# Scaling whole tiles with one VectorE instruction, empty instructions at ScalarE's head, and the first two loads on SyncE, in a row softmax on one core

## The chip, the cores and the metric

The kernel runs on one core of a Trainium2 chip. VectorE, ScalarE and SyncE are engines of the core, each with its own program; ScalarE and SyncE here also issue the transfers, each to a queue of its own. The metric is the device time of one execution in microseconds. The trace also gives a span, from the first to the last instruction of the program; the time is 1.7 to 1.8 us above it in every run here.

## The reference

The input is 16 x 1024 x 512 fp32, seen as 16,384 rows of 512. Each row gets a softmax of x / 2:

```python
x_scaled = x / 2.0
x_max = np.max(x_scaled, axis=-1, keepdims=True)
exp_x = np.exp(x_scaled - x_max)
return (exp_x / np.sum(exp_x, axis=-1, keepdims=True)).astype(np.float32)
```

That is 33.55 MB in and 33.55 MB out, and little arithmetic for each byte.

## The kernel before

Each of the 128 partitions holds 128 rows, in ten tiles: one of 3 rows, one of 7, seven of 15 and a last one of 13. In SBUF they lie in one arena of 100 rows, so tiles 8 and 9 reuse the places of earlier tiles and wait for their stores. Below, "row" is a row of 512 within a partition.

```python
PLAN = [
    ([3], 0), ([4, 3], 3), ([5] * 3, 10), ([5] * 3, 25), ([5] * 3, 40), ([5] * 3, 55),
    ([5] * 3, 70), ([5] * 3, 85), ([5] * 3, 0), ([5, 4, 4], 15),
]                       # chunks of each tile, and its place in the arena
LAG = 2                 # a chunk is scaled two chunks after its maximum
FUSED = {1, 2, 3}       # tiles that one tensor_mul scales per chunk
```

SyncE loads tile 0; ScalarE loads the rest. Tile 1's load is in three pieces: all but its last row, then the last row of 126 partitions, then that of two.

```python
if t == 0:
    nc.sync.dma_start(out=sb(t), in_=dram(xf, t)).then_inc(ld[t], 16)
elif t == SPREAD:                       # SPREAD = 1
    r = tiles[t][1] - 1
    for p, q, lo, hi in ((0, P, 0, r), (0, 126, r, r + 1), (126, P, r, r + 1)):
        nc.scalar.dma_start(...).then_inc(ld[t], 16)
else:
    nc.scalar.dma_start(out=sb(t), in_=dram(xf, t)).then_inc(ld[t], 16)
```

VectorE takes the negated maximum of a chunk. ScalarE takes the exponential of each row in place and adds up its sum. VectorE then takes the reciprocals and scales, and SyncE stores a tile once all of it is scaled.

```python
def do_mul(k):
    ...  # reciprocal of the chunk's sums, waits for its exponentials
    if t in FUSED:
        nc.vector.tensor_mul(chunk, chunk, recip broadcast along the row)
        return
    for r in range(c):
        nc.vector.tensor_scalar_mul(out=arena[:, a + r], in0=arena[:, a + r],
                                    scalar1=recip[:, b + r : b + r + 1])
```

The loads of tiles 0 and 1 stand ahead of the barrier with which the program begins, all other work behind it.

## Time and profile before

| | before |
|---|---|
| time | 161.64 us (161.61 to 161.68, 3 runs) |
| span of the profiled run | 159.9 us |
| VectorE (DVE) busy | 131.6 us, last instruction over at 144.7 us |
| ScalarE (ACT) busy | 94.4 us |
| transfers | 67.1 MB, first packet at 1.0 us, last at 158.6 us |
| tiles 0, 1, 2 reach VectorE | 6.71, 9.39, 18.26 us |

In the profile's row of slices, a digit is a fortieth of the span and gives the busy share in tenths. A transfer counts from its issue on a sequencer (SPq or ACTq) to its landing, when all its engines have reported to its semaphore. Within the chain that ended last (start in us, length, what), the piece that stands out is a load:

```profile
94.63 32.69 DMA arena<-in_x_dram
127.32 0.02 issue
127.34 2.82 DVE negmax L105
```

The last tile's load was issued at 94.63 and landed 32.7 us later; behind it come 17 us of VectorE and the last store. So loads, VectorE's tail and stores are linked here, with the transfers full throughout.

### The profile page before, as it was taken

To read this page: it belongs to the slowest core of one execution; us is meant where nothing else is said; L and a number is where in the kernel's file an instruction comes from. 1 tells how busy PE (TensorE), PEld (TensorE's weight loads), DVE (VectorE), ACT (ScalarE), POOL (GpSimd) and SP (SyncE) were. 2 spreads that over 40 slices of the span, in tenths; PEclk is the share of its full clock that TensorE was granted. 3 is DMA by queue.
4 is the path that set the end of the run, shared out by engine and by line. 5 is a ranking of instruction groups with operands and counts; after the bars stand their busy time and mean duration, and the time that the engine had idled before them with its cause. 6 is when DMAs were issued, how large, how long until landed. Compare 5 with 4: busy or idle time off the path is not lost.

```text
span 159.9 us, 476 instructions
## 1 busy us (share of the span) xinstructions
DVE 131.6 (82%) x153; ACT 94.4 (59%) x257; POOL 0.2 (0%) x4
## 2 busy tenths in 40 slices
DVE  0376499999999999999999999999999799992000
ACT  0369176768448547766688666786667948650000
POOL 0000000000000000000000000000000000000000
DMA  7998999999998989899999999998999998989993
GB/s 278 466 396 377 447 424 407 446 475 376 418 484 377 484 377 484 377 484 407 448 423 446 423 438 453 402 461 387 452 448 438 396 484 377 484 384 476 431 426 133
DMA packets 3028, 67.13 MB, mean 420 GB/s; under 512 B 337, under 2 KB 337, under 8 KB 721
## 3 DMA queue, kind: packets, MB, share of 16 engines
q1 hardware_dynamic: 1584, 34.34, 50.1%
q10 hardware_dynamic: 1440, 32.77, 48.1%
q14 instruction: 4, 0.02, 0.0%
HBM read 33.55 MB, written 33.55 MB: 420 GB/s over the span
## 4 chain that ended last, share of the span: by engine, by line
DVE 58%; DMA 31%; issue 0%; DVEq 0%; ACT 0%
DMA arena<-in_x_dram 31%; DVE negmax L105 30%; DVE arena L125 13%; DVE arena L118 13%; DVE recip L114 1%; DVEq L218 0%; ACT arena L144 0%
## 5 line engine op out<-in xcount | busy, mean ns | idle before, releaser
L144 ACT ACTIVATE arena<-arena,negmax 128x512 f32<-128x512 f32 x128 | 90.7, 710 | 42.5 <-DVE negmax L105 42.5
L105 DVE TENSOR_REDUCE negmax<-arena 128x5 f32<-128x2560 f32 (+2 forms) x27 | 72.1, 2675 | 12.2 <-DMA arena<-in_x_dram 12.2
L125 DVE TENSOR_SCALAR arena<-arena,recip 128x512 f32<-128x512 f32 x91 | 37.8, 482 | 0.7
L144 ACT ACTIVATION_READ_ACCUMULATOR arena<-arena,negmax 128x1 f32 x128 | 23.9, 187 | 0.0
L118 DVE TENSOR_TENSOR arena<-arena,recip 128x2560 f32<-128x2560 f32 (+2 forms) x8 | 21.0, 2625 | 0.3
L114 DVE RECIPROCAL recip<-sums 128x5 f32<-128x5 f32 (+2 forms) x27 | 4.8, 176 | 0.0
L144 ACT ACT_TABLE_LOAD x1 | 1.3, 1283 | 5.0 <-issue 5.0
L207 POOL MEMSET const-bfloat16-1.0<- 128x1 bf16 x1 | 0.1, 103 | 0.0
L207 POOL MEMSET const-uint8-127<- 128x1 uint8 x1 | 0.1, 103 | 0.0
L207 POOL MEMSET const-float32-1.0<- 128x1 f32 x1 | 0.1, 100 | 0.0
L207 POOL MEMSET const-float32-0.0<- 128x1 f32 x1 | 0.1, 99 | 0.2 <-issue 0.2
## 6 DMA issues: line engine op xcount, KB each, us to landing
arena<-in_x_dram ACTq DMA_DIRECT2D x7, 3840.0 KB, 42.9
out_dram<-arena SPq DMA_DIRECT2D x7, 3840.0 KB, 24.0
arena<-in_x_dram ACTq DMA_DIRECT2D x1, 3328.0 KB, 32.7
out_dram<-arena SPq DMA_DIRECT2D x1, 3328.0 KB, 14.2
out_dram<-arena SPq DMA_DIRECT2D x1, 1792.0 KB, 17.0
arena<-in_x_dram ACTq DMA_DIRECT2D x1, 1536.0 KB
arena<-in_x_dram SPq DMA_DIRECT2D x1, 768.0 KB, 6.7
out_dram<-arena SPq DMA_DIRECT2D x1, 768.0 KB, 15.5
```

The lines of the kernel that those rows point to most:

```text
L105: nc.vector.reduce_max(out=negmax[:, b : b + c], in_=arena[:, a : a + c], axis=mybir.AxisListType.X, negate=True,)._wait_ge(ld[t], 48 if t ...
L114: nc.vector.reciprocal(out=recip[:, b : b + c], in_=sums[:, b : b + c])._wait_ge(s_exp, k + 1).then_inc(s_rec, 1)
L118: nc.vector.tensor_mul(out=arena[:, a : a + c], in0=arena[:, a : a + c], in1=recip[:, b : b + c].unsqueeze(2).to_broadcast([P, c, D]),)._w ...
L125: ins = nc.vector.tensor_scalar_mul(out=arena[:, a + r], in0=arena[:, a + r], scalar1=recip[:, b + r : b + r + 1],)
L144: ins = nc.scalar.activation(out=arena[:, a + r], in_=arena[:, a + r], func=mybir.ActivationFunctionType.Exp, bias=negmax[:, b + r : b + r ...
L207: nc = _bacc.Bacc("TRN2", target_bir_lowering=False, num_devices=1)
```

## The change

The intent, as the code shows it: fewer and larger instructions on VectorE (a maximum for 8 or 7 rows instead of 5, one scaling instruction for a tile, two for the last), both first tiles loaded from one queue, ahead of the others, and ScalarE held back a little by 48 empty instructions, so that the first tiles have the transfer engines to themselves. A tile in PLAN now has the chunks for its maxima, the groups that one instruction scales, and its place. The diff, cut to its core (constants that stand twice in it are shown once):

```diff
 PLAN = [
-    ([3], 0), ([4, 3], 3), ([5] * 3, 10), ([5] * 3, 25), ...
+    ([3], [3], 0), ([4, 3], [7], 3), ([8, 7], [15], 10), ([8, 7], [15], 25),
+    ([8, 7], [15], 40), ([8, 7], [15], 55), ([8, 7], [15], 70), ([8, 7], [15], 85),
+    ([8, 7], [15], 0), ([5, 4, 4], [9, 4], 15),
 ]
+AHEAD = 48
+FIRST = 2
...
-            if t == 0:
-                nc.sync.dma_start(out=sb(t), in_=dram(xf, t)).then_inc(ld[t], 16)
-            elif t == SPREAD:
+            queue = nc.sync if t < FIRST else nc.scalar
+            if t == SPREAD:
...
+            for p, q, lo, hi in parts:
+                queue.dma_start(...).then_inc(ld[t], 16)
...
-    def do_mul(k):
-        t, b, c, a = chunks[k]
+    def do_mul(j):
+        t, b, c, a, k = groups[j]
...
-        for r in range(c):
-            ins = nc.vector.tensor_scalar_mul(...)
+        nc.vector.tensor_mul(
+            out=arena[:, a : a + c],
+            in0=arena[:, a : a + c],
+            in1=recip[:, b : b + c].unsqueeze(2).to_broadcast([P, c, D]),
+        )._wait_ge(s_rec, j + 1).then_inc(s_mul, 1)
...
-    issue_loads(0, 2)
+    issue_loads(0, FIRST)
+    for _ in range(AHEAD):
+        nc.scalar.nop()
```

## The prediction

> **What bounds the kernel now.** I read the page first: busy shares, the 40 slices, HBM bytes.
>
> ```profile
> span 159.9 us, 476 instructions
> DVE 131.6 (82%) x153; ACT 94.4 (59%) x257; POOL 0.2 (0%) x4
> DMA  7998999999998989899999999998999998989993
> HBM read 33.55 MB, written 33.55 MB: 420 GB/s over the span
> ```
>
> The row of DMA tenths is full from the second slice to the last but one, while VectorE has 28 us to spare: the transfers are the bound. Next the stages, cut by time (columns: window, length, busy us of DVE, ACT, POOL, clock, DMA share, GB/s).
>
> ```profile
> 2.00:6.00 4.00, 0.00 (x0) 1.00 (x1) 0.00 (x0) 1.00 1.05 427
> 42.00:127.00 85.00, 83.67 (x103) 61.09 (x169) 0.00 (x0) 1.00 1.00 432
> 127.00:154.00 27.00, 17.23 (x31) 10.25 (x29) 0.00 (x0) 1.00 1.01 436
> ```
>
> In the middle DVE is busy 98% too, so it is a close second; but DVE ends at 144.7 and stores alone fill the last 14 us. That backlog is DVE's slack. The 67.1 MB at 432 GB/s take 155.3 us, so a perfect start could win only about 2 us of 161.6. Third, the DVE rows by shape, and its first waits.
>
> ```profile
> L105 DVE TENSOR_REDUCE negmax<-arena 128x5 f32<-128x2560 f32 x22 | 61.9, 2813 | 4.6 <-DMA arena<-in_x_dram 4.6
> L125 DVE TENSOR_SCALAR arena<-arena,recip 128x512 f32<-128x512 f32 x91 | 37.8, 482 | 0.7
> L118 DVE TENSOR_TENSOR arena<-arena,recip 128x2560 f32<-128x2560 f32 x6 | 16.9, 2825 | 0.2
> ...
> 6.71 1.75 DVE L105 TENSOR_REDUCE negmax<-arena 128x3 f32<-128x1536 f32 x1 [6.71 <-DMA arena<-in_x_dram]
> 9.39 3.94 DVE L105 TENSOR_REDUCE negmax<-arena 128x4 f32<-128x2048 f32 x2 [0.93 <-DMA arena<-in_x_dram]
> 18.26 2.82 DVE L105 TENSOR_REDUCE negmax<-arena 128x5 f32<-128x2560 f32 x1 [3.53 <-DMA arena<-in_x_dram]
> ```
>
> Tiles 0, 1 and 2 reach DVE at 6.7, 9.4 and 18.3 us. Last, the DMA queues while both have work. q1 is SyncE's, q10 ScalarE's. At 2.5 to 5.5 us it is load against load, at 18 to 29 us the store of tile 0 (rows of 6,144 bytes) against loads (rows of 30,720).
>
> ```profile
> q10 hardware_dynamic: 68, 0.84, 68.3%
> q1 hardware_dynamic: 65, 0.40, 32.8%
> ...
> q10 hardware_dynamic: 144, 3.93, 82.8%
> q1 hardware_dynamic: 137, 0.79, 17.1%
> out_dram<-arena SPq DMA_DIRECT2D x1, 768.0 KB, 15.5
> ```
>
> The columns are packets, MB, share. The **packet counts** of the two queues are equal, 68 to 65 and 144 to 137, while the bytes follow the row size. So a queue with small rows gets few bytes: tile 0's store needed 15.5 us for 0.79 MB.
>
> **What the Trainium skill says.** "DMA: Bandwidth & Descriptors", section "Queues, rings and completion order": an engine round-robins between queue rows at packet granularity. The counts above agree; where the page expects some 9 to 17 descriptors in a packet, this trace has one row per packet. The same page, "Why a DMA increments its semaphore by 16 and not by 1", says a copy is split over the largest number of engines up to 16 that divides its row counts: 126 rows on 14 engines, 2 rows on 2. The program's split of tile 1's last row matches; no view names the engines. "VectorE: DVE Perf Modes", section "The perf-mode tier table (the rule you actually need)": fp32 tensor_scalar in SBUF runs at 2x, tensor_tensor at 1x. The trace agrees: five L125 take 2.07 us, one L118 of the same data 2.82 us.
>
> **The change part by part.**
>
> *1. The 48 empty instructions.* The build drops them: the built program of the changed kernel has no such instruction and the same order as one built with none. Effect 0. They would have held ScalarE's loads back behind SyncE's; that is lost.
>
> *2. Scaling and chunks.* The reduces of 5, 4 and 3 rows last 2813, 2281 and 1747 ns in the table by shape, so a row of 512 costs 0.533 us; from start to start one of 5 takes 2.73 (18.26 to 20.99), so 0.07 comes on top. The tensor_tensor has the same slope (2825, 2292, 1757) and 0.08 on top; a reciprocal takes 0.20. After tile 0's reduce the new DVE program holds:
> - reduces: 125 rows x 0.533 + 19 instructions x 0.07 = 68.0 us
> - scaling: 128 rows x 0.533 + 11 x 0.08 = 69.1 us
> - 11 reciprocals x 0.20 = 2.2 us
>
> That is **139.3 us**. The 91 rows that were scaled one by one cost 0.40 each (five from 65.06 to 67.04) and now 0.533, so +12 us; 16 fewer reciprocals and 7 fewer reduces give back 3.7. A full tile costs 4.34 + 3.80 + 0.20 + 8.08 = 16.4 us of DVE against 18.2 us of DMA (7.86 MB at 432 GB/s), so DVE still keeps up in the middle, but the slack at the end is nearly used.
>
> *3. Both first tiles on SyncE.* This is the part I expect to decide. SyncE's program now runs four issues before the barrier. From the durations seen (0.38, 0.38, 0.66, 0.25 with gaps of 0.04) it is through at 1.8 instead of ScalarE's 1.48, so tile 2's load is issued at about 2.28 (1.97 before). ScalarE's first load had its first packet 2.2 us after its issue (packet records: issued 0.12, data 2.30), so tile 2's packets begin near 4.5 us. By then tile 0 is done: 0.29 MB by 2.2 us in the queue view, the other 0.50 MB at 0.41 MB per us, so 3.4 us. Of tile 1's eight 12,288-byte packets per engine (0.46 us each) two to three are through. From there on every tile-1 packet takes turns with one 30,720-byte packet of tile 2 and then of tile 3, which needs 1.14 us (128 of them in the 9.1 us of 3.93 MB at 432 GB/s, eight per engine):
> - 5 packets left of the main part: 5 x (1.14 + 0.46) = 8.0, to 12.5 us
> - then its completion packet, 9 packets of 2,048 bytes, a completion packet and, on two engines, the two-row piece with its completion: 13 turns x 1.14 + 10 x 0.08 = 15.6, to **28 us**
>
> The check on this: tile 0's store has 8 data packets of 0.23 and one completion per engine, so 8 x 1.37 + 1.14 = 12.1 us from its first packet at 18.0; its last engine reported at 30.3. In the kernel before, tile 1 was ahead of tile 2 in one queue and was there at 9.4.
>
> *The sum.* DVE runs in program order; everything after tile 0's reduce, even tile 0's scaling, stands behind tile 1. So DVE idles from about 6 to 28 us and then works without a gap: 28 + 139.3 = 167.3. I checked tiles 8 and 9: their loads are issued near 76 and 109 us, after stores that have landed by then, and are needed at 128 and 145 us. The last store (3.41 MB, nothing left to share with) takes 1.0 to its first byte, 7.9 at 432 GB/s and 0.4 to report: 9.3, so 176.6. The end took 1.0 (158.93 to 159.9), which gives a span of 177.6. The time is 1.7 above the span (161.64 against 159.9): **179 us**.
>
> **Rivals.**
> - *Tile 1 is early after all.* If the empty instructions do reach the chip and last about 0.1 us each, or if a small row is not made to wait a turn, tile 1 lands near 8. Then DVE starts freely only with tile 2 at 17 to 18 us and has 133.5 us from there (139.3 less 5.8 of tile 1's reduces, tile 0's scaling and reciprocal): 18 + 133.5 + 9.3 + 1.0 + 1.7 = 163.5, or 162.5 with tile 2 at 17. Within 2%. For it speaks that somebody put the empty instructions there; against it the built program and the equal packet counts.
> - *Small rows share a turn.* If two 2,048-byte rows go in one turn, the tail has some five turns fewer, tile 1 lands near 22.5 and the time is 173.5. No view shows 2,048-byte rows competing, so I keep this in the range.
> - *DMA stays the bound and hides the rest* (161 to 162): this needs a DVE chain that ends by about 149, so tile 1 by 10. It is the old bound, and part 3 takes it away.
> - *Faster.* Tile 0 comes earlier (about 4 us, was 6.7), but tile 2 cannot come more than some 1.5 us earlier, and DVE has more work. I see no way to 2%.
>
> **Range and chances.** The end moves one to one with tile 1's arrival. With 22 to 31 us for it, and 1 us for the rest, the time is 172 to 183; I stretch the low side to 169 for a shorter tail or a later tile 2. The first rival has about 9%, faster 1%, slower the rest.
>
> **What would show it.** Right: tile 1's first reduce starts near 28 us with a DVE wait of about 20 us on a load; queue q1 moves little over 100 GB/s after 5 us and less later; after that DVE has no wait over 1 us to its end near 167; the scaling rows of 7680 elements take about 8.1 us; the DMA row has gaps late in the run; loads of ScalarE start at 2.3 us. Wrong: many empty instructions on ScalarE or loads issued after 5 us; tile 1's reduce before 12 us; a DVE wait on tiles 8 or 9; DVE ending much before the last store is issued.

## The result, and the profile after

The changed kernel takes **176.88 us** (median of 4 runs, 176.11 to 178.01); the kernel before takes 161.66 beside it. The ratio is 1.0947, with a 95% interval of 1.0888 to 1.1007. Ratios here are the mean time of one kernel's fast runs over that of the other's from the same rounds, so not quite the ratio of the medians. The output is correct.

The page of the changed kernel, the lines that answer to those of before:

```profile
span 175.1 us, 365 instructions
DVE 141.2 (81%) x42; ACT 92.8 (53%) x257; POOL 0.2 (0%) x4
DMA  7999999999999999999989999999397059559795
HBM read 33.55 MB, written 33.55 MB: 383 GB/s over the span
```

The transfers now have holes in the last third, and VectorE was busy for only 10 us more while the span grew by 15. No empty instructions ran: the trace has 365 instructions, 111 fewer than before, and VectorE alone has 111 fewer (42 for 153). ScalarE's 257 would not show it, since they leave out what only a sequencer runs. The timeline of VectorE (start, length, instruction, idle time ahead of it and what ended it) shows where it stood idle:

```profile
4.47 1.75 DVE L129 TENSOR_REDUCE negmax<-arena 128x3 f32<-128x1536 f32 x1 [4.47 <-DMA arena<-in_x_dram]
25.03 3.95 DVE L129 TENSOR_REDUCE negmax<-arena 128x4 f32<-128x2048 f32 x2 [18.81 <-DMA arena<-in_x_dram]
...
30.77 8.21 DVE L129 TENSOR_REDUCE negmax<-arena 128x8 f32<-128x4096 f32 x2
...
162.55 2.29 DVE L141 TENSOR_TENSOR arena<-arena,recip 128x2048 f32<-128x2048 f32 x1
```

Tile 0 arrives 2.2 us earlier than before. Tile 1, used at 9.39 before, is there only at 25.0, and VectorE waits 18.8 us for it. Tile 2 lands at 17.9 us, so at 30.8 there is nothing to wait for any more. VectorE then runs without a gap to 164.8. The stages (window, length, busy us of DVE, ACT, POOL, clock, DMA share, GB/s) say the same from the other side:

```profile
12.00:24.00 12.00, 0.00 (x0) 0.00 (x0) 0.00 (x0) 1.00 1.01 410
78.00:122.00 44.00, 43.90 (x12) 30.12 (x85) 0.00 (x0) 1.00 1.01 427
122.00:164.00 42.00, 41.86 (x14) 22.04 (x62) 0.00 (x0) 1.00 0.65 280
```

From 12 to 24 us no engine computes while the transfers are busy with later tiles. From 122 us on, the loads are all in and the stores wait for VectorE, which is busy 41.9 of 42 us: the bound has moved to it. The scaling and reduce rows by shape:

```profile
L141 DVE TENSOR_TENSOR arena<-arena,recip 128x7680 f32<-128x7680 f32 x7 | 57.1, 8158 | 0.2
L129 DVE TENSOR_REDUCE negmax<-arena 128x8 f32<-128x4096 f32 x7 | 30.9, 4412 | 0.0
```

A scaled row now costs 8158 / 15 = 544 ns, where single ones took 0.40 us each from start to start.

### The profile page after: what moved, and what is told of

It is laid out like the page before. It is cut to its first block, busy times and chain, and to the rows that moved or that the text cites. A ratio compares the mean times of both kernels' runs of the same rounds, so it can differ in the third digit from the quotient of the medians.

```text
span 175.1 us, 365 instructions
## 1 busy us (share of the span) xinstructions
DVE 141.2 (81%) x42; ACT 92.8 (53%) x257; POOL 0.2 (0%) x4
## 4 chain that ended last, share of the span: by engine, by line
DVE 80%; DMA 13%; SPq 1%; issue 0%
DVE arena L141 40%; DVE negmax L129 39%; DMA arena<-in_x_dram 13%; DVE recip L138 1%; SPq L123 1%
## 5 line engine op out<-in xcount | busy, mean ns | idle before, releaser
L129 DVE TENSOR_REDUCE negmax<-arena 128x8 f32<-128x4096 f32 (+4 forms) x20 | 70.4, 3558 | 23.3 <-DMA arena<-in_x_dram 23.3
L141 DVE TENSOR_TENSOR arena<-arena,recip 128x7680 f32<-128x7680 f32 (+4 forms) x11 | 70.0, 6364 | 0.4
L138 DVE RECIPROCAL recip<-sums 128x15 f32<-128x15 f32 (+4 forms) x11 | 2.4, 220 | 0.0
```

The source lines that it names most:

```text
L129: nc.vector.reduce_max(out=negmax[:, b : b + c], in_=arena[:, a : a + c], axis=mybir.AxisListType.X, negate=True,)._wait_ge(ld[t], 48 if t ...
L138: nc.vector.reciprocal(out=recip[:, b : b + c], in_=sums[:, b : b + c])._wait_ge(s_exp, k).then_inc(s_rec, 1)
L141: nc.vector.tensor_mul(out=arena[:, a : a + c], in0=arena[:, a : a + c], in1=recip[:, b : b + c].unsqueeze(2).to_broadcast([P, c, D]),)._w ...
```

## The experiments

All of them ran beside the kernel before, which took 161.7 us in each set. A run that took over 1.5% longer than the fastest of its kernel is called slow and left out. The theory: packets of the two queues take turns, so moving tile 1's small rows to the queue beside ScalarE's long rows makes it late, and its arrival sets the end. The rivals: the new scaling costs the time; SyncE's queue is slow in itself; the empty instructions act.

### Tile 1 back on ScalarE's queue

```diff
-FIRST = 2
+FIRST = 1
```

> The changed kernel, but tile 1 is loaded by ScalarE's queue again, ahead of tile 2 (only tile 0 on SyncE). My theory (the queues take turns packet by packet, so tile 1 on the other queue comes late): tile 1 is there near 9.4 us and tile 2 near 18.2, VectorE ends near 152, time 163 to 164.5, the cost of the longer scaling alone being 1 to 2 %. Rival (the new scaling and its larger chunks cost the 15 us by themselves): time stays at 175 to 178.

Measured: 165.0 us (164.4 to 166.6, 4 runs), ratio 1.022 (1.016 to 1.028).

```profile
9.36 3.94 DVE L129 TENSOR_REDUCE negmax<-arena 128x4 f32<-128x2048 f32 x2 [3.20 <-DMA arena<-in_x_dram]
...
18.24 8.21 DVE L129 TENSOR_REDUCE negmax<-arena 128x8 f32<-128x4096 f32 x2 [3.06 <-DMA arena<-in_x_dram]
```

Both arrivals are as foretold, and VectorE ends at 152.3. The time is half a us over the stretch named (the profiled run, 164.4, lies in it). So the larger part, 12 of the 15 us, goes with the queue of one tile; the scaling with its larger chunks costs 3.3 us by itself.

### The old VectorE program with both first tiles on SyncE

```diff
-            if t == 0:
-                nc.sync.dma_start(...)
...
+            queue = nc.sync if t < 2 else nc.scalar
...
+                queue.dma_start(...)
```

> The kernel before, with one thing of the change: both first tiles on SyncE. My theory: tile 1 arrives near 25 us as in the changed kernel; VectorE's older program needs some 130.5 us after that (68.5 of reduces, 20.4 and 36.1 of scaling, 5.5 of reciprocals), so 25 + 130.5 + 12 = 167.5 us. Rival (scaling is the cause, the queue is harmless): 161.7.

Measured: 168.7 us (168.56 to 169.0), ratio 1.044 (1.042 to 1.046).

```profile
24.75 3.95 DVE L104 TENSOR_REDUCE negmax<-arena 128x4 f32<-128x2048 f32 x2 [18.59 <-DMA arena<-in_x_dram]
```

The late tile is there without the new scaling, at the same moment. VectorE needs 130.6 us from there (to 155.3), as summed. The last store took 10.4 us instead of 9.3 from its issue, which is most of the 1.2 us over the forecast. The two halves cost 3.3 and 7.0 us alone and 15.2 together. That they don't add up fits the slack: the kernel before could have issued its last store some 4.9 us later at no cost (it landed at 158.9, and a last store alone needs 9.3, so it could have been issued at 149.6 instead of 144.8; an estimate). In the profiled runs VectorE's end moved by 7.6, 10.6 and 20.1 us; less 4.9 this is 2.7, 5.7 and 15.2, where the times moved by 2.7, 6.9 and 15.2. The longer last store is the 1.1 us that is missing in the second.

### Tile 1 as one transfer

```diff
-SPREAD = 1
+SPREAD = -1
```

> The changed kernel, but tile 1 is one transfer of 128 rows of 14,336 bytes instead of three transfers (12,288, then 2,048 bytes a row). Same bytes, 9 turns per engine instead of up to 21. My theory (a packet costs a turn whatever its size): tile 1 arrives near 13 us instead of 25, time 163.5 to 166. Rival (SyncE's queue gets a fixed low share of the bytes): tile 1 arrives near 25 as before, time 175 to 178.

Measured: 168.7 us (167.5 to 168.8), ratio 1.042 (1.038 to 1.045).

```profile
16.80 3.95 DVE L129 TENSOR_REDUCE negmax<-arena 128x4 f32<-128x2048 f32 x2 [10.49 <-DMA arena<-in_x_dram]
```

The same bytes on the same queue land 8 us earlier once they are fewer packets, so the rival of a fixed share of bytes is out. The edit also takes two issues from ahead of the barrier, so ScalarE's loads are issued at 1.25 instead of 2.20 us; that works against an early tile 1. My 13 us was too early, and the time with it 2.7 us over the stretch named: thirteen of the 16 engines reported between 13.6 and 13.9 us, but one at 15.3 and two near 16.8, which were one and two turns behind. The wait ends only when the last engine has reported, and I had not counted on one that is two turns behind.

### Shorter rows on the other queue

```diff
-                parts = ((0, P, 0, tiles[t][1]),)
+                n = tiles[t][1]
+                parts = ((0, P, 0, 8), (0, P, 8, n)) if t in HALVED else ((0, P, 0, n),)
```

Here HALVED is {2, 3}, and their semaphores are awaited at 32. Nothing on SyncE's queue or on VectorE differs from the changed kernel.

> The changed kernel, but tiles 2 and 3 are loaded in two transfers each, of 8 and of 7 rows, so ScalarE's packets beside tile 1 are 16,384 or 14,336 bytes (about 0.57 us) instead of 30,720 (1.14 us). Nothing on SyncE's queue and nothing on VectorE changes, and the bytes are the same. My theory (tile 1 pays one packet of the other queue for each of its own): its remaining 18 or so turns are 0.57 us shorter each, so it lands near 25 - 18 x 0.57 = 15, at most 18.5 us, and time = arrival + 151.9 = 167 to 170.5. Rival (tile 1 is late because SyncE's queue is slow or has low rank, or because of its own small rows): tile 1 still near 25 us, time 176 to 178.

Measured: 168.8 us (168.7 to 168.9), ratio 1.044 (1.042 to 1.045). The queue views (queue: packets, MB, share of 16 engines), first of the changed kernel from 12 to 18 us, then of this one from 10 to 16 us:

```profile
q10 hardware_dynamic: 88, 2.21, 89.5%
q1 hardware_dynamic: 77, 0.15, 6.7%
```

```profile
q10 hardware_dynamic: 159, 2.16, 92.1%
q1 hardware_dynamic: 134, 0.24, 10.9%
...
17.03 3.95 DVE L132 TENSOR_REDUCE negmax<-arena 128x4 f32<-128x2048 f32 x2 [10.81 <-DMA arena<-in_x_dram]
```

In both stretches tile 1's small rows are on their way. ScalarE's queue moves the same MB in six microseconds, in nearly twice as many packets, and SyncE's queue gets nearly twice as many of its own through. (It has somewhat fewer, as not all 16 engines have rows of tile 1 to the end.) Tile 1 lands at 17.0 instead of 25.0. This is the cleanest test of the theory: nothing of tile 1 was touched, only the length of what it takes turns with.

### No empty instructions, and instructions that are kept

```diff
-AHEAD = 48
+AHEAD = 0
```

> The changed kernel with the number of empty instructions set to 0. My theory: the built program has the same instructions in the same order, so the same time, 176 to 178 us. Rival (the empty instructions act): another time by more than 1 %.

Measured: 176.7 us (176.6 to 176.8), the same as with 48 of them (176.9), and the trace again has 365 instructions. The build drops them. The time alone wouldn't show it: the next run keeps 48 instructions and its time is nearly the same.

The second kernel has drains in their place, which also give the engine nothing to compute, but which the build keeps:

```diff
-        nc.scalar.nop()
+        nc.scalar.drain(fusable=False)
```

> The changed kernel with 48 drain instructions, which the build keeps, in the place of the 48 empty ones, which it drops. On an idle ScalarE each should be little more than its issue slot, an estimate of 0.04 to 0.1 us from the gaps between short sequencer instructions in the trace. My theory: the barrier and ScalarE's loads come later by what 48 of them take beyond SyncE's 1.98 us; with 0.04 us each almost nothing changes (tile 1 near 24 us, time 175 to 177); with 0.1 us each the loads are issued near 5 us, tile 1 lands near 9 to 10 and the time is 164 to 166. Either way tile 1's arrival, not the instructions, sets the time: time = arrival + 151.5 to 152.5 unless arrival is under 14. Rival (instructions at the head of the program matter through the fetching of the program): time moves by several us while tile 1's arrival doesn't.

Measured: 177.8 us (177.8 to 178.4), 0.8 us over the stretch for short drains, with tile 1 used at 25.7 instead of near 24. The first line of its profile counts them too:

```profile
span 176.0 us, 413 instructions
```

They stand 0.033 us apart in the trace and are over at 1.70 us, before SyncE's four issues (through at 1.75, its drain at the barrier at 2.01). (The next expectation has 0.035 and 1.74, which takes in ScalarE's own drain at the barrier.) So even 48 empty instructions that were kept would have held nothing back, if they are as short.

> The changed kernel with 140 drains in the place of the empty instructions. The run with 48 showed them 0.035 us apart, over at 1.74 us, before SyncE was through its four issues. 140 of them should end near 5.0 us, ScalarE's loads be issued near 5.4, their first packets come near 8 to 9 us, tile 1 land at 8.5 to 10 and tile 2 near 18.5: time 164 to 167, as with tile 1 on ScalarE's queue. Rival (the hold at the head doesn't help unless it is tied to the data): tile 1 over 14 us, time over 167.

With 140 drains: 165.3 us (165.1 to 165.4 in the three fast runs; one slow run of 169.9 is left out), ratio 1.021 (1.020 to 1.023). ScalarE's first load is issued at 5.5 us.

```profile
9.32 3.95 DVE L129 TENSOR_REDUCE negmax<-arena 128x4 f32<-128x2048 f32 x2 [2.03 <-DMA arena<-in_x_dram]
```

A hold of the right length does bring tile 1 in on time. It also delays the barrier for all engines, and tile 0's reduce with it (5.5 us).

### ScalarE waits for tile 0 instead

```diff
+    nc.scalar.wait_ge(ld[0], 16)
     issue_loads(FIRST, len(tiles))
```

> The changed kernel, and ScalarE waits for tile 0 to have landed (near 4.5 us) before it issues its loads, which is what empty instructions of the right length would do. My theory: tile 1 is nearly through before tile 2's first packet, lands near 8.5 to 9.5, tile 2 near 17.5 to 18.5, time 162.5 to 164.5: VectorE's longer program is what is left. Rival (both first tiles on one queue are slow in themselves): tile 1 stays late, time over 170.

Measured: two fast runs, 164.5 and 164.8 us, ratio 1.018 (1.016 to 1.020). Two more runs, the profiled one among them, were slow (169.7 and 170.1) and are not used. One fast time is at the upper end of the stretch named and one 0.3 us over it, both far under the rival's 170, with two runs alone behind this. No fast run of it was profiled, so tile 1's arrival is not shown for it.

### Looking for a version that beats both

> The kernel before with both first tiles on SyncE and ScalarE waiting for tile 0 before its loads: the head of the change as it was meant, with the older, shorter VectorE program. My theory: tile 1 near 9.2 and tile 2 near 18.3 us as in the kernel before, transfers are the bound again, 161.3 to 162.3 us, the same as before. Rival (an earlier tile 0, at 4.5 instead of 6.7 us, is worth something): under 161.

The old VectorE program with this head takes 161.73 us (5 runs, ratio 1.000, 0.999 to 1.001). Tile 0 is there at 4.5 instead of 6.7 us, but the time is the same: the transfers bind. Tile 1 was used at 11.1 us instead of the 9.2 forecast, because one engine reported at 11.1 and all others by 8.8; it wasn't followed up and cost nothing here.

> The kernel before with tile 1 as one transfer of 14,336-byte rows on ScalarE's queue instead of three transfers. In its trace the rate falls to 320 to 350 GB/s from 8 to 9.5 us, where the 2,048-byte rows end and the long rows start, some 0.4 MB or 0.8 us. If the small rows cause the dip: tile 2 lands up to 0.8 us earlier and the time is 160.9 to 161.4. If not: 161.7, or slower by the few tenths for which the split was once made.

The kernel before with tile 1 in one piece takes 161.38 us (6 runs, 161.29 to 162.28, ratio 0.999, 0.998 to 1.001). The dip at 8 to 9.5 us is gone (about 430 GB/s in the packet records, against 317 to 346) and tile 2 is used at 17.8 instead of 18.3, but the time isn't lower beyond the noise; five of the six runs are between 161.29 and 161.49.

> The kernel before with both first tiles on SyncE, ScalarE waiting for tile 0 before its loads, and tile 1 in one piece: the best of each part. The transfers are the bound; the dip of some 0.4 us at 8 to 9.5 us should be gone as in the one-piece variant of the kernel before. 161.2 to 161.6 us, so at best 0.3 % under the kernel before; under 160.8 would show that an earlier tile 0 is worth something.

Both together: 161.55 us (5 runs, ratio 0.999, 0.998 to 1.000). No version tried is clearly faster than the kernel before.

## Why the prediction was right or wrong

It was right, in the mechanism too: 179 us was forecast with a range of 172 to 183, stretched to 169 at the low side, and 176.9 was measured.

- **The empty instructions** have no effect, shown by the 365 instructions in the traces with and without them, where 48 that are kept make 413.
- **VectorE's program** after tile 0 was summed to 139.3 us and took 139.8 (25.03 to 164.84). Its reading of five L125 against one L118 (2.07 against 2.82 us) bears out the 2x and 1x that it cites in direction alone: the ratio is 1.4, with five instructions against one.
- **The turns.** That packets take turns whatever their size is shown by shortening either side: tile 1 lands at 16.8 or 17.0 instead of 25.0. One term was mis-sized: tile 2's packets were to begin at 4.5 us, 2.2 us after their issue as ScalarE's first load in the kernel before, and began at 5.7, 3.5 us after the issue at 2.20. Why they took longer isn't known. Until then tile 1 was alone: of its 128 large packets 27 were through at 4.5 us (1.7 for each of 16 engines, where two to three were counted) and 66 at 5.7 (4.1 each). So about 4 were left to take turns instead of 5, two errors that partly cancel, and they were over at about 9.4 to 11.4 us instead of 12.5. From there to 25.0 it took 13.6 to 15.6 us, where 15.6 were forecast. The records name no engine, so how much of the 3 us between 28 and 25 belongs to each part stays open.
- **Small rows sharing a turn**, kept in the range, did not come: from 12 to 24 us the trace has 139 packets of SyncE's queue and 168 of ScalarE's. (By the prediction's own sum its time is 22.5 + 151.3 = 173.8, not 173.5.)
- **One to one.** Time less the moment at which tile 1 is used is 151.9, 151.9, 151.9, 151.9 and 152.0 us in the profiled runs of the changed kernel, of the one without empty instructions, with tile 1 in one piece, with short rows and with 48 drains. The sum gave 151.3.
- **The first rival** ("tile 1 is early after all") did not come, but it forecast 163.5 for a head that works. The runs with tile 1 early and the new scaling took 165.0 (on ScalarE's queue), 165.3 (140 drains) and 164.5 and 164.8 (the wait).
- **Why VectorE's small rise in work cost so little before and so much here:** it fits within the slack as long as VectorE starts on time. This was argued from the ends of VectorE. It agrees within 0.2 us with the profiled runs of the four kernels (neither half of the change, each alone, both), once the longer last store of one is counted; no run took the slack away by itself.

What stays open, besides the late start of tile 2's packets, is why the changed kernel's time scatters by 1.9 us (176.1 to 178.0) where the kernel before scatters by 0.1 beside it. A turn more or less for the slowest engine would be 1.2 us; it wasn't isolated.

## What to carry to other kernels

On two queues that share the transfer engines, count packets and not bytes: here a transfer of short rows beside one of long rows was served about one short row per long one (77 against 88 packets in six microseconds). So put what is needed first at the head of the same queue as what follows (tile 1 at 9.4 instead of 25.0 us), or hold the other queue back by a wait on data (164.5 and 164.8 instead of 176.9 us). Don't cut an urgent load into small pieces when another queue is busy (tile 1 in one piece came at 16.8). Look in the built program whether an instruction that is there for its delay is still there.

## What the Trainium skill lacked or had wrong

- "DMA: Bandwidth & Descriptors", section "Queues, rings and completion order", gives some 9 to 17 descriptors for a packet. Here every row of 2,048 to 30,720 bytes was a packet of its own and cost a turn: 88 packets against 77 in the same six microseconds, with 2.21 against 0.15 MB. The page doesn't draw the consequence for the order of loads.
- The same page, section "Issuing engines are not separate DMA queues", says that several issuing engines only save the time to issue. Moving one load of 1.8 MB from ScalarE to SyncE moved its use from 9.4 to 25.0 us and the time from 165.0 to 176.9.
- The same page, section "Latency and other measured facts", has about 600 ns to the first byte. Here the first packet came 1.0 us after the start of the issuing instruction on an idle machine, and 0.65 us after its end, which may be what the page means. What it lacks is the case of a busy other queue: 3.5 us from the start (2.20 to 5.7).
- No page has how close drains follow each other on ScalarE: 48 of them stood 0.033 us apart. No page says that empty instructions may be missing from the built program (365 instructions with 48 of them and with none).
